# Where hidden tiles lie and in which order contraction tiles are taken, in a two-layer RetNet and GLA trunk

## The chip, the cores and the metric

The kernel runs on one core of one Trainium2 chip. The metric is the device time of an execution in microseconds, the median of several runs.

## The reference

A trunk of two layers on 512 tokens of width 1024, with 16 learned meta tokens ahead of them (528 columns). Each layer is a half-step SwiGLU FFN (hidden width 2816), a mixer, and another half-step FFN, each behind an RMSNorm; layer 0 mixes by retention (4 heads, keys of 256, values of 512), layer 1 by gated linear attention (GLA). Cut to what matters here:

```python
for i in range(2):
    h = h + 0.5 * swiglu(rmsnorm(h, norm_ffn1[i]), ffn1_w_in[i], ffn1_w_out[i])
    hn = rmsnorm(h, norm_mix[i])
    h = h + (retention(hn, ...) if i == 0 else gla(hn, ...))
    h = h + 0.5 * swiglu(rmsnorm(h, norm_ffn2[i]), ffn2_w_in[i], ffn2_w_out[i])

def swiglu(x, w_in, w_out):
    gate, up = split(x @ w_in, 2)
    return (silu(gate) * up) @ w_out

def retention(h, w_in, head_norm, w_out):       # per head, decayed and causal
    q, k, v, g = split(h @ w_in)
    q, k = rotary(q), rotary(k) / 16
    o = rmsnorm(((q @ k.T) * decay) @ v, head_norm)
    return (o * silu(g)) @ w_out
```

## The kernel before

Everything lies transposed: channels on the 128 partitions, the 528 tokens in the free dimension, in two halves of 264. A "row tile" is 128 channels.

Every product is made in float32r from split operands. `mm3` (L472) issues three matmuls for one contraction tile: the weight's high part with the moving operand's high and low part (L473, L474), then the weight's low part with the high part again (L475). A matmul has a 128x128 weight and 264 moving columns (256 in the last FFN). Weights come from HBM, and ACT and DVE split each into high and low part some tiles ahead (L167, L168).

Most projections are made as "units": two row tiles of the output and two token halves by a Strassen-like scheme of seven products instead of eight. `unit_steps` (L667) issues them in the order of `Weights.UNIT` (L75), each over the contraction tiles that `ks` names, in the order given. The moving operand of a product is either a quarter of the input itself (n11, n21, n22) or a precomputed sum of quarters (t1, t2, n3, t4):

```python
    UNIT = ("a11", "s1", "s2", "a12", "s3", "s4", "a22")
    WITH = {"a11": ("n11", "X"), "s1": ("t1", "Z"), "s2": ("t2", "X"), "a12": ("n21", "Q"), "s3": ("n3", "X"),
            "s4": ("n22", "Z"), "a22": ("t4", "X")}
```

X is a PSUM bank that several products of a unit use one after another, with an ACT copy of it in between; Q and Z are the two banks of one accumulator.

An input projection contracts over 4 pairs of row tiles, so a product has 4 x 3 = 12 matmuls and a unit 84. Its inputs are u (`Split`, L401; quarters at a pitch `HP_` of 288 floats, k after k) and the sums in `th`, `tl` (L768 to L770 in an FFN, L1209 to L1211 in the retention; `[P, 4, 4, 288]`, the slot ahead of the contraction tile). `FLIP` (32 floats) lies between high and low parts. `rows4` (L709) gives the contraction tiles as 0, 1, 2, 3.

An FFN makes hidden row tiles in pairs (f, f+1), in three groups (`GROUPS`, L30): f = 0 to 6, 8 to 12, 14 to 20, so 4, 3 and 4 hidden tiles; the last FFN has four groups. A hidden tile holds seven quarters high and seven low. `h_tile` (L778) places it in one of four buffers H0 to H3, by a count of the tiles made so far. `hidden` (L823) fills it from the gated rows; for f = 0 and 2 it is put off (`todo`, L1041 to L1049), so that in the FFNs with three groups the tiles of the first group are made in the order f = 0, 4, 2, 6. H0 to H3 also hold, at the start of an FFN, temporary sums (H0, H1) and the normalized and gated rows of f = 0 and 2 (H2, H3; `place`, L783). `unit_o` (L981) is a unit of a group's out product; it sorts the group's tiles by f, and contracts over them as 0, 1, 2, 3, or, where the group has four tiles and the product's slot is odd, as `ODD` = 1, 0, 3, 2 (L59, L987). The out product of a group runs after the first gate unit of the next.

The retention (L1200) runs head by head: q and k (`rope`, units but in head 0), the out product of the head before, the values (`rv`, units but in head 0), scores and transposes, gates (`rg`, two units in every head), and the product with the values (`pv`). The out product, `out_steps` (L1062), makes 8 row tiles, each in two token halves over 4 contraction tiles (the four value tiles of the head), plain, without sums: 8 x 2 x 4 x 3 = 192 matmuls. Its input `og` has a pitch of 288 floats between halves and 608 between contraction tiles (L1476). The last head's is made with `part=2`: the first two row tiles take their first two contraction tiles before all else.

The framework's scheduler fixes the order of instructions on each engine when the kernel is built, from program order and priorities (`urgent`, L450); on the chip each engine runs its own list in order.

Of the kernel before, what the change touches and what calls it, by code (L numbers as in the profile page):

```python
# [11 lines left out]
F32R = mybir.dt.float32r  # L12
# [4 lines left out]
P = 128  # L17
# [16 lines left out]
HALVES = ((0, 264), (264, 528))  # L34
# [24 lines left out]
ODD, BACK = (1, 0, 3, 2), 48  # L59
# [180 lines left out]
def trunk(ctx, tc, a):  # L240
# [8 lines left out]
    W = Weights(tc, ctx)  # L249
# [200 lines left out]
    def urgent():  # L450

        return tc.high_priority(offset=HEAD_START)
# [183 lines left out]
    def width(halves):  # L636
        return halves[0][1] - halves[0][0]
# [71 lines left out]
    def rows4(what):  # L709
        return range(4)  # L710

    def unit(key, name, order, halves, ks, rhs, place, row1, c22, c21, behind=None):
        wd = width(halves)

        def places():
            X = bank(f"X{name}")[:, :wd]
            QZ = acc_tile(f"QZ{name}")[:, :, :wd]
            su = place()
            return X, QZ, su[:, :2], su[:, 2:]

        for st in unit_steps(key, name, order, halves, ks, rhs, places, row1, c22, c21, behind):
            st()
# [30 lines left out]
    def ffn(which, layer, halves, gcol, u, feed, late=False):  # L753


        me = f"{which}{layer}"
# [4 lines left out]
        with tc.tile_pool(name=f"h_{me}", bufs=1) as hp, tc.tile_pool(name=f"t_{me}", bufs=1) as tp, \  # L761
# [3 lines left out]
            HW = 14 * pitch + flip  # L765
# [5 lines left out]
            places = [lambda i=i: tp.tile([P, 4, HT], F32, tag=f"t{i}", name=f"sz{me}") for i in "hl"]  # L771
            th, tl = [[t[:, :, k, :wd] for k in range(4)] for t in (th, tl)]
            rhs_in = quarters(halves, u, th, tl)
            H, normed, made = {}, {}, [0]
            place_of = [spare() if feed else in_turn([lambda: tp.tile([P, 4, wd], F32, tag="su", name=f"su{me}", bufs=3)])]
            groups = GROUPS if feed else LAST_GROUPS

            def h_tile(name):  # L778

                made[0] += 1  # L780
                return hp.tile([P, HW], F32R, tag=f"H{(made[0] - 1) % 4}", name=name)

            def place(j):  # L783

# [38 lines left out]
            def hidden(f, y, part=None):  # L823

                gi = [g[0] <= f < g[1] for g in groups].index(True)
                if feed is None and gi == len(groups) - 1:
                    h = h_tile(f"h{me}{f}")[:, BACK:]
                    h = [[h[:, q * 2 * wd:q * 2 * wd + T] for q in (i, i + 2)] for i in (0, 1)]
                    h = [list(t) for t in zip(*h)]
                    for i in range(2):  # L830
                        split(pair(h[0][i], halves), pair(h[1][i], halves), y[:, 2 - 2 * i:4 - 2 * i])
                elif part == 1:
                    (hi, lo), t = h, _ = halfway.pop()
                    with urgent():
                        split(hi[:, :2], lo[:, :2], y[:, :2])
                    V.tensor_sub(t[0][:, 0], y[:, 1], y[:, 3])
                    split(hi[:, 3], lo[:, 3], t[0][:, 0])
                    V.scalar_tensor_tensor(t[1][:, 1], y[:, 0], -1.0, t[1][:, 0], ALU.mult, ALU.subtract)
                    split(hi[:, 6], lo[:, 6], t[1][:, 1])
                else:  # L840
                    h = h_tile(f"h{me}{f}")
                    hi, lo = h = [h[:, o:o + 7 * pitch].rearrange("p (q t) -> p q t", q=7)[:, :, :wd]
                                  for o in (0, 7 * pitch)]
                    t = t_pair(tmp, ("hf", "hf"), f"{me}h{f}", wd)
                    if part is None:
                        t_sums(t, y[:, 1:3], y[:, 3], y[:, 0])
                        split(hi[:, :3], lo[:, :3], y[:, :3])
                        for i in range(2):
                            split(hi[:, 3 + 2 * i:5 + 2 * i], lo[:, 3 + 2 * i:5 + 2 * i], t[i])
                    else:  # L850
                        with urgent():

                            split(hi[:, 2], lo[:, 2], y[:, 2])
                            V.tensor_sub(t[0][:, 1], y[:, 2], y[:, 3])
                            split(hi[:, 4], lo[:, 4], t[0][:, 1])
                            V.scalar_tensor_tensor(t[1][:, 0], y[:, 1], -1.0, t[0][:, 1], ALU.mult, ALU.subtract)
                            split(hi[:, 5], lo[:, 5], t[1][:, 0])
                        halfway.append((h, t))
                H.setdefault(gi, {})[f] = h
# [29 lines left out]
            turn = [0]  # L889
# [125 lines left out]
            for n, (kind, a_, b_) in enumerate(steps):  # L1015
                if kind == "p":
                    s, f = a_, b_
# [44 lines left out]
    def out_steps(name, key, hh, hl, halves, scale, feed, per=1, part=None):  # L1062


        nk, wd = len(hh), width(halves)
        ws, ps = {}, {}

        def products(d, k0, k1):
            if d // per not in ws:
                ws[d // per] = W.get(key(d // per))  # L1070
            if k0 == 0:
                ps[d] = acc_tile(f"po_{name}{d}")
            for hf, (r0, r1) in enumerate(halves):
                for k in range(k0, k1):
                    mm3(ps[d][:, hf, :wd], *W.at(ws[d // per], ((d % per) * nk + k) * P),
                        hh[k][:, r0:r1], hl[k][:, r0:r1], k == 0, k == nk - 1)
                if k1 == nk:
                    if hf == len(halves) - 1 and d % per == per - 1:
                        W.free(ws[d // per])
                    hook()  # L1080

        def step(d):
            if part and d == 0:
                for i in range(2):
                    products(i, 0, part)
            products(d, part if part and d < 2 else 0, nk)
            xv = x[d][:, halves[0][0]:halves[-1][1]].rearrange("p (b t) -> p b t", t=wd)
            with urgent():
                ins = V.scalar_tensor_tensor(xv, ps[d][:, :len(halves), :wd], scale, xv, ALU.mult, ALU.add)
            if feed:  # L1090
                feed(d, ins)

        return [lambda d=d: step(d) for d in range(KD)]
# [106 lines left out]
    def retention(u, feed):  # L1200
        with tc.tile_pool(name="retp", bufs=1) as rp, tc.tile_pool(name="wmore", bufs=2) as wp, psum_pool(4) as pp:
# [11 lines left out]
            rhs_u = quarters(HALVES, u, th, tl)  # L1213
            place = spare()
            causal = rp.tile([P, P], F32, tag="causal", name="causal")
            nc.sync.dma_start(causal, a["tri"][1])
            og, normed, tabs = {}, {}, {}
# [32 lines left out]
            def head(h):  # L1250
                qk = {}

                def rope_pair(s):


                    t = [(rp if s == "k" else tmp).tile([P, T], F32, tag=f"gs{m}" if s == "k" else "sg",
                                                        name=f"rt{s}{h}{m}") for m in range(2)]

                    def row1(ab, qz):
                        V.tensor_add(pair(t[0], HALVES), ab, qz)  # L1260

                    def c22(c, s_):
                        V.tensor_add(t[1][:, b0:b1], c, s_)

                    def c21(c):
                        S.copy(t[1][:, a0:a1], c)

                    j = (0 if s == "q" else 8) + 2 * h
                    unit(("rqk", j), f"rqk{s}{h}", W.UNIT, HALVES, rows4, rhs_u, place, row1, c22, c21)
                    cos, sin = [tabs[s][:, c, :] for c in range(2)]  # L1270
                    pa, pb = [tmp.tile([P, T], F32, tag="hf", name=f"r{i}{s}{h}") for i in "ab"]
                    V.tensor_mul(pa, t[0], cos)
                    V.tensor_mul(t[0], t[0], sin)
                    V.tensor_mul(pb, t[1], sin)
                    V.tensor_add(pa, pa, pb)
                    qk[s, 0], qk[s, 1] = [[rp.tile([P, T], F32R, tag=f"{s}{i}{m}", name=f"{s}{i}{m}_{h}")
                                           for i in range(2)] for m in range(2)]
                    S.copy(qk[s, 0][0], pa)
                    V.tensor_mul(t[1], t[1], cos)
                    V.tensor_sub(t[0], t[0], t[1])  # L1280
                    V.tensor_sub(qk[s, 0][1], pa, qk[s, 0][0].bitcast(F32))
                    split(qk[s, 1][0], qk[s, 1][1], t[0])
# [35 lines left out]
                def values():  # L1318
# [18 lines left out]
                    for m0 in (0, 2):  # L1337
                        vt.extend(rp.tile([P, T], F32, tag=f"gs{m0 + i}", name=f"vt{h}{m0 + i}") for i in range(2))

                        def row1(ab, qz, m0=m0):  # L1340
                            V.scalar_tensor_tensor(pair(vt[m0], HALVES), ab, -1.0, qz, ALU.mult, ALU.subtract)

                        def c22(c, s, m0=m0):
                            V.tensor_add(vt[m0 + 1][:, b0:b1], c, s)

                        def c21(c, m0=m0):
                            S.copy(vt[m0 + 1][:, a0:a1], c)

                        unit(("rv", h, m0), f"rv{h}{m0}", W.UNIT, HALVES, rows4, rhs_u, place, row1, c22, c21)

                def turn(j):
                    if not v:
# [61 lines left out]
                def gates(m0, use):  # L1414
# [16 lines left out]
                        S.activation(o, c, AF.Silu)  # L1431
                        use(m0 + 1, a0, a1, o)

                    unit(("rg", h, m0), f"rg{h}{m0}", W.UNIT, HALVES, rows4, rhs_u, place, row1, c22, c21)
                    sgs.extend(mine)

                def pv(into):
# [782 lines left out]
```

## Time and profile before

| | |
|---|---|
| median of 3 runs | 2061.5 us (2060.38 to 2062.69) |
| profiled execution | 2058.71 us |
| its span, first to last instruction | 2056.9 us |
| granted TensorE clock, mean | 0.997 |
| PE busy | 2030.9 us, 99% |
| DVE busy | 1795.5 us, 87% |
| ACT busy | 1199.0 us, 58% |

The page lists busy time by engine over one profiled execution. PE is the matmuls, PEld the weight loads that overlap them. Successive matmuls overlap too, each showing about 0.28 us from its start to its modelled end while they start some 0.12 us apart: "busy" says that PE has work, not that it works at its best. A timeline row has the start in us from the span's start, the duration, engine, source line, operation, and written and read tiles. A row of the table of windows has the stretch, its length, then each engine's busy time and number of instructions in it, the granted clock, and the share and rate of DMA.

### The profile page before, as it was taken

The numbers are of one execution on the slowest core, as the hardware profiler recorded it, in microseconds if no ns is written. First come the engines' busy times: TensorE is split into PE (matmuls) and PEld (weight loads), VectorE is DVE, ScalarE is ACT, GpSimd is POOL, SyncE is SP. The second block draws the span as 40 slices with busy tenths as digits, with TensorE's granted clock in tenths as the row PEclk, the third lists the DMA queues.
The fourth block names the chain that finished last, engine by engine and source line by source line (L and its number), as shares of the span: only waits on it lengthen the run. The fifth ranks groups of instructions, "written<-read, shape, count | busy, mean of one in ns | idle before, by whom it ended". The sixth has DMA issues, their size and how long they took to land. (4 is left out here: it accounts for less than half of the span.)

```text
span 2056.9 us, 43086 instructions
## 1 busy us (share of the span) xinstructions
PE 2030.9 (99%) x16335; PEld 1973.7 (96%) x16335; DVE 1795.5 (87%) x3299; ACT 1199.0 (58%) x2435; POOL 210.4 (10%) x181
## 2 busy tenths in 40 slices
PE   8999999999999999999999999999999999999998
PEld 8999999999999999999999999999999988999998
DVE  8988999978787889988889998999997968999996
ACT  5656666554545465656666665666745445666664
POOL 1011110010101000111111011111001000111110
PEclk9999999999999999999999999999999999999999
DMA  6576776455555532776776377677614351686872
GB/s 203 155 188 169 188 186 169 139 134 144 140 140 136 142 107 68 187 190 153 196 204 170 95 198 182 153 204 180 199 53 123 89 165 58 161 214 171 194 180 73
DMA packets 176112, 318.85 MB, mean 155 GB/s; under 512 B 17568, under 2 KB 40736, under 8 KB 175904
## 3 DMA queue, kind: packets, MB, share of 16 engines
q1 hardware_dynamic: 133856, 237.04, 35.3%
q0 software_dynamic: 40896, 75.51, 23.4%
q10 hardware_dynamic: 1152, 3.55, 0.5%
q8 instruction: 128, 2.10, 0.4%
q14 instruction: 80, 0.66, 0.1%
HBM read 311.76 MB, written 4.26 MB: 154 GB/s over the span
## 5 line engine op out<-in xcount | busy, mean ns | idle before, releaser
L167 ACT CAST whi<-raw 128x512 fp32r<-128x512 f32 (+1 forms) x893 | 525.3, 606 | 458.6 <-DVE raw L173 107.0
L168 DVE TENSOR_TENSOR wlo<-raw,whi 128x512 fp32r<-128x512 f32 (+1 forms) x893 | 586.2, 670 | 136.0 <-ACT whi L167 120.0
L167 ACT CAST whi<-pair 128x512 fp32r<-128x512 f32 (+1 forms) x304 | 183.9, 605 | 95.4 <-ACT su L695 12.7
L168 DVE TENSOR_TENSOR wlo<-pair,whi 128x512 fp32r<-128x512 f32 (+1 forms) x304 | 202.1, 665 | 5.8 <-ACT whi L167 5.0
L136 POOL DMA_DIRECT2D pair<-in_f_in x73 | 89.0, 1220 | 729.6 <-DVE wlo L168 333.4
L173 DVE TENSOR_TENSOR raw<-pair,raw 128x512 f32<-128x512 f32 (+1 forms) x146 | 97.4, 667 | 2.6
L175 DVE TENSOR_TENSOR raw<-raw,raw 128x512 f32<-128x512 f32 (+1 forms) x146 | 97.3, 667 | 2.5
L136 POOL DMA_DIRECT2D pair<-in_f_out x44 | 53.5, 1216 | 367.6 <-DVE wlo L168 120.5
L474 PE MATMUL po_r<-ogl,whi 128*128 128x264 f32 x256 | 72.1, 281 | 0.0
L473 PE MATMUL po_r<-ogh,whi 128*128 128x264 f32 x256 | 72.0, 281 | 0.0
L475 PE MATMUL po_r<-ogh,wlo 128*128 128x264 f32 x256 | 71.7, 280 | 0.0
L136 POOL DMA_DIRECT2D pair<-in_ret_in x20 | 24.4, 1222 | 297.6 <-DVE wlo L168 102.6
L473 PE MATMUL Xf10o<-hf,whi 128*128 128x264 f32 x176 | 50.7, 288 | 0.9 <-DVE x L1003 0.3
L473 PE MATMUL Xf20o<-hf,whi 128*128 128x264 f32 x176 | 50.6, 287 | 0.7 <-DVE x L1003 0.3
L473 PE MATMUL Xf11o<-hf,whi 128*128 128x264 f32 x176 | 50.4, 286 | 0.7 <-ACT hf L506 0.3
L474 PE MATMUL Xf10o<-hf,whi 128*128 128x264 f32 x176 | 49.5, 281 | 0.0
L474 PE MATMUL Xf20o<-hf,whi 128*128 128x264 f32 x176 | 49.5, 281 | 0.0
L474 PE MATMUL Xf11o<-hf,whi 128*128 128x264 f32 x176 | 49.5, 281 | 0.0
L475 PE MATMUL Xf10o<-hf,wlo 128*128 128x264 f32 x176 | 49.2, 281 | 0.0
L475 PE MATMUL Xf20o<-hf,wlo 128*128 128x264 f32 x176 | 49.2, 280 | 0.0
L475 PE MATMUL Xf11o<-hf,wlo 128*128 128x264 f32 x176 | 49.1, 280 | 0.0
L473 PEld LDWEIGHTS po_r<-ogh,whi 128*128 128x128 f32 x256 | 48.1, 188 | 0.0
(1172 smaller groups left out, 8515.6 us busy)
## 6 DMA issues: line engine op xcount, KB each, us to landing
raw<-in_f_in SPq DMA_DIRECT2D x277, 256.0 KB, 4.0
pair<-in_f_in SPq DMA_DIRECT2D x150, 256.0 KB, 4.3
pair<-in_f_in POOLq DMA_DIRECT2D x73, 512.0 KB, 6.8
raw<-in_f_out SPq DMA_DIRECT2D x80, 256.0 KB, 3.6
raw<-in_ret_in SPq DMA_DIRECT2D x76, 256.0 KB, 3.5
raw<-in_f_out SPq DMA_DIRECT2D x72, 192.0 KB, 3.2
pair<-in_f_out SPq DMA_DIRECT2D x48, 256.0 KB, 3.8
pair<-in_f_out POOLq DMA_DIRECT2D x24, 512.0 KB, 6.0
```

The costliest lines, as they stand in the source:

```text
L136: nc.gpsimd.dma_start(t, aps[2].unsqueeze(1).broadcast_to([P, 2, n]), accum_op=ALU.add)
L167: self.nc.scalar.copy(hi[:, :n], raw)
L168: V.tensor_sub(lo[:, :n], raw, hi[:, :n].bitcast(F32))
L173: V.tensor_add(s2, self.tiles[c][:, 1], self.tiles[c, "a11"])
L175: V.tensor_add(raw, raw, s2)
L473: nc.tensor.matmul(ps, lhsT=lh, rhs=rh, start=start, stop=False, **kw)
L474: nc.tensor.matmul(ps, lhsT=lh, rhs=rl, start=False, stop=False, **kw)
L475: return nc.tensor.matmul(ps, lhsT=ll, rhs=rh, start=False, stop=stop, **kw)
```

## The change

Three things. A hidden tile's buffer follows its row tile, `f // 2 % 4`, instead of a count of tiles made. Units of the retention take the contraction tiles in the order 1, 0, 3, 2 in the four products whose moving operand is a sum (t1, t2, n3, t4). And an out product with four contraction tiles takes them as 1, 0, 3, 2 in its second token half. Only the retention's has both; GLA's has one half.

```diff
     def rows4(what):
         return range(4)
 
+    def rows4_odd(what):
+        return range(4) if what[0] == "n" and what != "n3" else ODD
+
...
-            H, normed, made = {}, {}, [0]
+            H, normed = {}, {}
...
-            def h_tile(name):
+            def h_tile(f):
 
-                made[0] += 1
-                return hp.tile([P, HW], F32R, tag=f"H{(made[0] - 1) % 4}", name=name)
+                return hp.tile([P, HW], F32R, tag=f"H{f // 2 % 4}", name=f"h{me}{f}")
...
-                    h = h_tile(f"h{me}{f}")
+                    h = h_tile(f)
...
             for hf, (r0, r1) in enumerate(halves):
-                for k in range(k0, k1):
+                turn = ODD if hf and nk == len(ODD) else range(nk)
+                for k in turn[k0:k1]:
                     mm3(ps[d][:, hf, :wd], *W.at(ws[d // per], ((d % per) * nk + k) * P),
-                        hh[k][:, r0:r1], hl[k][:, r0:r1], k == 0, k == nk - 1)
+                        hh[k][:, r0:r1], hl[k][:, r0:r1], k == turn[0], k == turn[-1])
...
-                    unit(("rqk", j), f"rqk{s}{h}", W.UNIT, HALVES, rows4, rhs_u, place, row1, c22, c21)
+                    unit(("rqk", j), f"rqk{s}{h}", W.UNIT, HALVES, rows4_odd, rhs_u, place, row1, c22, c21)
```

The units `rv` (L1349) and `rg` (L1434) change in the same way as `rqk` (L1269).

More of the change, by code (lines that the diff above doesn't have):

```diff
@@ L826, in hidden @@
                 if feed is None and gi == len(groups) - 1:
-                    h = h_tile(f"h{me}{f}")[:, BACK:]
+                    h = h_tile(f)[:, BACK:]
                     h = [[h[:, q * 2 * wd:q * 2 * wd + T] for q in (i, i + 2)] for i in (0, 1)]
@@ L1347, in c21 @@
                             S.copy(vt[m0 + 1][:, a0:a1], c)
-                        unit(("rv", h, m0), f"rv{h}{m0}", W.UNIT, HALVES, rows4, rhs_u, place, row1, c22, c21)
+                        unit(("rv", h, m0), f"rv{h}{m0}", W.UNIT, HALVES, rows4_odd, rhs_u, place, row1, c22, c21)
                 def turn(j):
@@ L1432, in c21 @@
                         use(m0 + 1, a0, a1, o)
-                    unit(("rg", h, m0), f"rg{h}{m0}", W.UNIT, HALVES, rows4, rhs_u, place, row1, c22, c21)
+                    unit(("rg", h, m0), f"rg{h}{m0}", W.UNIT, HALVES, rows4_odd, rhs_u, place, row1, c22, c21)
                     sgs.extend(mine)
```

## The prediction

> **What bounds the kernel now.** The page first: one line for the span and one for each engine's share of it.
>
> ```profile
> span 2056.9 us, 43086 instructions
> PE 2030.9 (99%) x16335; PEld 1973.7 (96%) x16335; DVE 1795.5 (87%) x3299; ACT 1199.0 (58%) x2435; POOL 210.4 (10%) x181
> ```
>
> PE is busy 99% of the span, so time comes off the end only where the matmuls themselves get closer together or a stop of PE goes. The profiled execution took 2058.7 us, 1.8 more than its span and 2.8 (0.14%) less than the median of the three runs, 2061.5. I make the sum as a difference against the profiled execution and carry it over to the median.
>
> A busy PE is not a PE at its best. The matmuls of a stage overlap, so what counts is the distance between starts, and the table of windows gives it: a window's length over the matmuls in it (the count in brackets has two or three more, which only reach into the window; I use the program's own count). I asked for the first head's value projection, the first out product of the retention, three value stages made of products of sums, the first-group out products of two FFNs, and a second-group one.
>
> ```profile
> core 0: us, PE busy (x) PEld busy (x) DVE busy (x) ACT busy (x) POOL busy (x), PEclk, DMA share, GB/s
> 385.35:407.75 22.40, 22.40 (x194) 22.40 (x193) 22.38 (x42) 11.88 (x25) 0.00 (x0) 1.00 0.20 63
> 468.34:491.22 22.88, 22.88 (x194) 22.88 (x193) 22.32 (x37) 7.82 (x15) 0.00 (x0) 1.00 0.27 87
> 491.22:511.19 19.97, 19.97 (x171) 19.97 (x169) 15.00 (x23) 11.05 (x23) 2.44 (x2) 1.00 0.72 189
> 592.44:612.40 19.96, 19.96 (x170) 19.96 (x169) 14.99 (x23) 11.05 (x23) 2.44 (x2) 1.00 0.73 188
> 694.01:713.98 19.97, 19.97 (x171) 19.97 (x170) 14.55 (x23) 11.19 (x23) 2.44 (x2) 1.00 0.72 178
> 874.41:914.97 40.56, 40.56 (x339) 40.56 (x338) 34.48 (x58) 21.97 (x43) 4.87 (x4) 1.00 0.77 192
> 975.23:1006.23 31.00, 31.00 (x254) 30.50 (x253) 27.67 (x55) 19.03 (x42) 3.66 (x3) 1.00 0.77 199
> 1218.31:1258.87 40.56, 40.56 (x339) 40.56 (x338) 34.48 (x58) 21.97 (x43) 4.87 (x4) 1.00 0.75 191
> ```
>
> All of these are 128x264 matmuls at a granted clock of 1.00. The first row is the yardstick: 192 matmuls (4 tiles, 2 halves, 8 contraction tiles, 3 each) in 22.40 us, 116.7 ns each, with DVE busy for 22.38 of it. The out product below has the same 192 matmuls of the same form, PE is busy all through, and it takes 22.88: 0.48 us more without a stop. A value stage, two units of 7 x 4 x 3 = 84 matmuls, should take 168 x 0.1167 = 19.60 and takes 19.97: 0.37 more. An out product of a first group, four units, should take 336 x 0.1167 = 39.20 and takes 40.56: 1.36 more.
>
> The timeline shows where such time lies. First a change of product in an FFN unit, then the start of the fourth row of the out product (24 matmuls a row from 468.34), then, in the second head's k unit, the product with u that follows one with the sums.
>
> ```profile
> 302.61 0.28 PE L474 MATMUL QZf10g<-ulf,whi 128*128 128x264 f32 x1
> 302.72 0.28 PE L475 MATMUL QZf10g<-uhf,wlo 128*128 128x264 f32 x1
> 302.84 0.28 PE L473 MATMUL Xf10g<-thf,whi 128*128 128x264 f32 x1
> 302.96 0.28 PE L474 MATMUL Xf10g<-tlf,whi 128*128 128x264 f32 x1
> ```
>
> ```profile
> 476.57 0.28 PE L473 MATMUL po_r<-ogh,whi 128*128 128x264 f32 x1
> 476.69 0.28 PE L474 MATMUL po_r<-ogl,whi 128*128 128x264 f32 x1
> 476.81 0.28 PE L475 MATMUL po_r<-ogh,wlo 128*128 128x264 f32 x1
> 476.92 0.28 PE L473 MATMUL po_r<-ogh,whi 128*128 128x264 f32 x1
> ...
> 478.02 0.28 PE L473 MATMUL po_r<-ogh,whi 128*128 128x264 f32 x1
> ```
>
> ```profile
> 563.60 0.28 PE L473 MATMUL QZrqkk<-uhret,whi 128*128 128x264 f32 x1
> ...
> 564.93 0.28 PE L475 MATMUL QZrqkk<-uhret,wlo 128*128 128x264 f32 x1
> 565.15 0.39 PE L473 MATMUL Xrqkk<-rth,whi 128*128 128x264 f32 x1
> 565.38 0.29 PE L474 MATMUL Xrqkk<-rtl,whi 128*128 128x264 f32 x1
> ```
>
> The FFN unit goes from u to t without a break. In the out product the starts are 0.117 apart up to 476.92, and the next nine distances take 1.10 instead of 1.05 us. The eleven distances of the k unit's product take 1.33 instead of 1.28. Nothing waits there; the matmuls are only further apart for a while.
>
> **What sets it.** The code's constants offer a reason. A quarter's pitch is 288 floats, 1152 bytes, or four and a half times 256; hi and lo parts lie a further 128 bytes askew; an H tile is 14 x 288 + 32 floats, again an odd number of 128 bytes. So every step from hi to lo, from one contraction tile to the next, and from one H tile to the next moves the start of PE's moving operand into the other 128-byte half of a 256-byte stretch. Call the halves A and B. I write down the halves in program order and count the places where one matmul starts in the half of the one before ("repeats").
>
> In the value projection of the first head and in FFN units (sums and u begin in the same half) there is none, and their rows are clean. In the out product, half 0 of a row runs A B A B over its four contraction tiles (within a tile A B A), half 1 lies one pitch on and runs B A B A: a repeat between the halves and one between rows, 2 x 8 = 16 a head, and 0.48 / 16 = 30 ns each. In a retention unit the sums must begin in the half in which u ends: then u to t1, t2 to u, u to n3, n3 to u, u to t4 and t4 to the next u repeat, 6 a unit, and 0.37 / 12 = 30 ns each. The same price out of two different stages is what makes me believe the counting. The third place is a first group. Its H tiles are made in the order f = 0, 4, 2, 6 and lie in H0 to H3 in that order, so sorted by f their halves are A A B B: two repeats in each product, 14 a unit, and with the odd slots' order 1, 0, 3, 2 four more between products, 18 a unit, 72 an FFN, and 1.36 / 72 = 19 ns each where they crowd.
>
> **The change, part by part.** It adds and removes no instruction; the same matmuls read other places or come in another order.
>
> *H tiles by row tile.* f = 0, 2, 4, 6 now lie in H0, H1, H2, H3: A B A B, and the odd slots, by 1, 0, 3, 2, as well. No repeat is left in 72. Group 1 has H0 to H2 and group 2 H3, H0, H1, H2 both before and after, and the last FFN makes its tiles in the order of f anyway, so there nothing moves. FFNs with this first group: three (layer 0's two, layer 1's first). Two rows show 1.36 each; the third has the same 336 matmuls and I give it the same: 3 x 1.36 = 4.08 us.
>
> *Products of sums in the retention.* t1, t2, t4 and n3 by 1, 0, 3, 2: where the sums begin in B, their products now start in A and end in B as those of u do. Heads 1 to 3 have six units each, head 0 two: 20 units x 6 x 30 ns = 3.65 us (20 x 0.37 / 2 is 3.7). All four sums are ready before the first unit, so the order opens no wait.
>
> *Second half of the retention's out product.* 1, 0, 3, 2 gives A B A B in both halves: 4 x 0.48 = 1.92 us. In the last head the first two rows take two contraction tiles ahead of the rest; the slice 1, 0 is the same pair, and the last tile to be ready (m = 3, first token half) is asked for in half 0 first, before and after. GLA's last out product also has four contraction tiles but a single half, and is not touched.
>
> Sum: 4.08 + 3.65 + 1.92 = 9.65 us.
>
> *What waits take back.* Heads 1 to 3 have stops in the q and k units, as at 564.93 above, where PE stands for its X bank until ACT has copied it. If such a stop goes back to work that DVE and ACT began at the end of the product before, PE only arrives earlier and stands longer, and repeats removed ahead of it are lost: up to the q unit's 6 and the k unit's 4, 0.3 us a head, 0.9 in all; if it moves along with PE, nothing. I take the 0.9, since these stages follow the busiest of DVE. The out product itself is safe: DVE's 22.32 us fit into the 22.40 that remain, and the first row above shows PE at full pace beside 22.38. In the first groups DVE goes from 34.48 / 40.56, 85%, to 34.48 / 39.20, 88%.
>
> Sum with that: 9.65 - 0.9 = 8.75 us. Profiled execution 2058.7 to 2049.95, median 2061.5 to 2052.75; I say 2052.7.
>
> The Trainium skill speaks against the whole of this: "SBUF — State Buffer", section "Who interferes with whom", gives PE two independent read ports, one for the moving operand and one for weight loads, and calls the port pair shared by VectorE and GpSimd the only place of contention; the order of contraction tiles would then be worth 0. This trace parts from it in the second row against the first.
>
> **The rivals.**
>
> *Stops come in place of the repeats* (chance 0.13). The second-group row is the model: 252 matmuls should take 29.40 us, 12 repeats add 0.36, and it takes 31.00, so 1.24 is stops, at DVE 27.67 / 31.00 = 89%. The first groups come to 88%. If they stopped as often, 1.24 x 336 / 252 = 1.65 each, 5.0 in all would go: 8.75 - 5.0 = 3.75, so 2057.7; in between where fewer come. Against it: the second group's hidden tiles are made right ahead of it with a narrower margin, and at 85% the first groups of two FFNs have no stop at all.
>
> *No effect* (0.05). The lost time would belong to something that stays, such as the change of the PSUM bank or weight tile at the start of a product: 2061.5. Every slow place above does lie behind such a change. Against it: the FFN unit at 302.84 and the value projection change both without a break. This is also where that section on SBUF would have it end.
>
> *Slower* (0.04). Gated tile f = 4 now goes to H2, where the normalized rows and the gated rows of f = 0 lie; its writing has to wait until the first hidden tile has been made from them, and ACT's weight casts, on which PE lives, are queued behind. It decides if that wait exceeds 8.75 / 3 = 2.9 us an FFN. At half a unit, 4.9 us, it gives 3 x 4.9 - 8.75 = +6, so 2067.5.
>
> ```profile
> 827.71 0.70 DVE L507 TENSOR_TENSOR hf<-t1f20h,hf 128x528 fp32r<-128x528 f32 x1
> 844.95 0.86 ACT L506 CAST hf<-su 128x792 fp32r<-128x792 f32 x1 [0.69 <-DVE su L970]
> ```
>
> The first row ends the tile of f = 0, the second begins that of f = 4, 16.5 us later. With such room I give it little; most of the 0.04 is an order of instructions that comes out otherwise.
>
> **How the numbers follow.** 0.78 for the sum, 0.13, 0.05 and 0.04 for the rivals. The forecast is the likeliest case. Its own lower end: nothing taken back, 2051.85, less the 1.1 us by which the fastest run lies under the median, 2050.7; I say 2050.5. The upper end goes into the first rival, to 2057.3, nearly its 2057.7. Outside lie 0.05 + 0.04, half of the first rival and a little of the first case, together under 0.2. A change under 0.2%, 4.1 us, can't be told from none here: the bound lies at 2057.4. Faster 0.78 and most of the first rival, 0.87; same 0.05 and the rest of it, 0.09; slower 0.04.
>
> **What would show it.** Right: the out products of the retention at 22.4 us each, first groups at 39.2, value stages at 19.6, the boundaries in the timeline as even as that at 302.84, and each later stage starting earlier by what has been saved so far. The first rival: those distances even, but new gaps of 0.2 us or more at X banks in the first groups. Wrong: 22.88 and 40.56 as before (then the halves are not the cause), or value stages above 19.97 (then the sums begin in the same half as u, and the new order makes the repeats that it should remove).

## The result, and the profile after

The changed kernel takes 2054.7 us in the median of five runs (2050.3 to 2055.6), the kernel before 2061.5, so 6.8 us less in the medians. The ratio, which is not that of the medians, is 0.9963 with a 95% interval of 0.9949 to 0.9978, 7.6 us. Two further sets of runs gave 0.9959 (0.9947 to 0.9972) each, 7.9 and 8.2 us in the medians. Its profiled execution has a span of only 3.1 us less than that of before, 2053.8 against 2056.9, although the matmuls' distances have gained three times as much. Both have to be explained. The page's first lines have the same instructions and the same work for DVE, and 4.8 us less of busy PE:

```profile
span 2053.8 us, 43086 instructions
PE 2026.1 (99%) x16335; PEld 1968.4 (96%) x16335; DVE 1794.8 (87%) x3299; ACT 1198.9 (58%) x2435; POOL 210.3 (10%) x181
```

First the distances. These are the windows of the changed kernel for the same eight stages, in the same order, as those quoted of the kernel before:

```profile
382.59:404.99 22.40, 22.40 (x194) 22.40 (x193) 22.38 (x42) 11.89 (x25) 0.00 (x0) 1.00 0.19 60
468.21:490.61 22.40, 22.40 (x194) 22.40 (x193) 22.26 (x37) 7.82 (x15) 0.00 (x0) 1.00 0.25 83
490.61:510.21 19.60, 19.60 (x170) 19.60 (x169) 15.06 (x24) 11.05 (x23) 2.44 (x2) 1.00 0.75 190
590.25:609.85 19.60, 19.60 (x171) 19.60 (x169) 15.11 (x24) 11.05 (x23) 2.44 (x2) 1.00 0.72 186
690.53:710.13 19.60, 19.60 (x170) 19.60 (x169) 14.45 (x23) 11.19 (x23) 2.44 (x2) 1.00 0.72 183
869.88:909.15 39.27, 39.27 (x338) 39.27 (x337) 34.05 (x58) 21.91 (x43) 4.87 (x4) 1.00 0.77 195
969.41:1000.41 31.00, 31.00 (x255) 30.54 (x254) 27.70 (x55) 19.07 (x42) 3.66 (x3) 1.00 0.77 201
1213.86:1253.12 39.26, 39.26 (x338) 39.26 (x337) 34.05 (x58) 21.89 (x43) 4.87 (x4) 1.00 0.79 202
```

The yardstick and the second group stay (22.40, 31.00); the retention's out product has gone from 22.88 to 22.40, each value stage from 19.97 to 19.60, the first groups from 40.56 to 39.27. That is 116.7 ns a matmul everywhere, to within 0.1 us. The timeline at the start of the fourth row of the out product, where nine distances had taken 1.10 us, now has nine in 1.05:

```profile
476.50 0.28 PE L475 MATMUL po_r<-ogh,wlo 128*128 128x264 f32 x1
476.61 0.28 PE L473 MATMUL po_r<-ogh,whi 128*128 128x264 f32 x1
...
477.66 0.28 PE L473 MATMUL po_r<-ogh,whi 128*128 128x264 f32 x1
```

Then what was taken back. The granted clock is 0.995 in this profile, 0.997 in that of before. The windows table finds it: PE ran at half clock for 6.8 us between the first head's scores and gates, and for 3.4 us at two later places at the start of a stage. The first row is the window ahead of the half-clock stretch; the last column but two is the granted clock.

```profile
404.99:412.20 7.21, 5.59 (x44) 5.20 (x43) 7.18 (x17) 6.37 (x16) 1.23 (x1) 1.00 0.67 150
412.20:419.00 6.80, 6.71 (x34) 6.54 (x33) 4.76 (x13) 2.90 (x11) 0.00 (x0) 0.50 0.09 16
1118.80:1122.20 3.40, 3.40 (x17) 3.40 (x17) 1.93 (x6) 0.62 (x1) 1.92 (x2) 0.50 0.85 220
1463.50:1466.90 3.40, 3.40 (x13) 2.92 (x12) 2.44 (x6) 1.77 (x3) 1.73 (x2) 0.51 1.08 245
```

In the kernel before, the scores and gates of the first head ran at full clock all through:

```profile
407.75:416.94 9.19, 7.15 (x58) 6.61 (x57) 8.90 (x21) 7.52 (x20) 1.23 (x1) 1.00 0.58 123
416.94:436.96 20.02, 20.02 (x172) 20.02 (x169) 14.98 (x28) 12.22 (x26) 1.23 (x1) 1.00 0.49 134
```

There the two stages take 29.21 us; in the changed kernel they take from 404.99 to 436.64, 31.65, so 2.4 us are lost although the gates lost their repeats. Setting the start of each stage in one trace against the other gives the account of the two profiled executions: first groups 2.57 + 1.29 + 1.30 = 5.2 us won, out products 1.8, value stages 1.1, q and k units 0.4, gates of heads 1 to 3 0.8, in all 9.3; head 0's scores and gates lose 2.4, the starts of two later stages 1.4 and 2.5, in all 6.3. The other stages differ both ways and about cancel (the most, 1.6 us, is won in the first FFN's plain up products, where the kernel before ran at half clock at 21 us); what is left, 3.0, is the difference of the spans, 3.1, to within 0.1.

### The profile page after: what moved, and what is told of

Its sections match the earlier page's. It is cut to its first block, busy times and chain, and to the rows that moved or that the text cites. A ratio compares the mean times of both kernels' runs of the same rounds, so it can differ in the third digit from the quotient of the medians.

```text
span 2053.8 us, 43086 instructions
## 1 busy us (share of the span) xinstructions
PE 2026.1 (99%) x16335; PEld 1968.4 (96%) x16335; DVE 1794.8 (87%) x3299; ACT 1198.9 (58%) x2435; POOL 210.3 (10%) x181
## 4 chain that ended last, share of the span: by engine, by line
PE 75%; DVE 16%; ACT 3%; issue 3%; DMA 2%; POOL 0%; SPq 0%; POOLq 0%; DVEq 0%; ACTq 0%
DVE wlo L168 5%; PE po_r L474 1%; PE po_r L475 1%; PE po_r L473 1%; ACT whi L167 1%; DVE hf L507 1%; PE Xf21o L473 1%; PE lv L1753 1%; PE Xf20o L473 1%; PE Xf20o L474 1%; PE Xf20o L475 1%; DVE unf L799 1%; PE Xf21o L475 1%; PE Xf21o L474 1%; PE Xf11u L473 1%
## 5 line engine op out<-in xcount | busy, mean ns | idle before, releaser
L474 PEld LDWEIGHTS po_r<-ogl,whi 128*128 128x128 f32 x256 | 48.0, 188 | 0.0
```

Of the source, the lines that this page charges most:

```text
L474: nc.tensor.matmul(ps, lhsT=lh, rhs=rl, start=False, stop=False, **kw)
```

## The experiments

The theory: a repeat of the 128-byte half costs 19 to 30 ns and the change removes some 400 of them (3 x 72 in the first groups, 20 x 6 in the units, 4 x 16 in the out products, by the prediction's count). The rivals: the loss belongs to the change of product, bank or weight (the prediction's "no effect"); the order of the weights, not the operand's place, makes the difference; or stops and half clock set the time. Every kernel is timed against the kernel before, with the ratio's 95% interval. Unless it says otherwise, nothing of the computation is left out.

**One part at a time, on the kernel before.** First the tiles: `h_tile(f)` with `tag=f"H{f // 2 % 4}"`, and nothing else of the diff.

> The kernel before with one part of the change: hidden tiles placed by their row tile. Theory (a repeat of the 128-byte half costs 19 to 30 ns): the out products of the three first groups go from 40.56 us to 39.2 where they had no stop, everything else keeps its distances (value stages 19.97, retention out products 22.88); 4.1 us under the kernel before at the same clock, and 5.2 if the 1.1 us of stops in the first FFN's first group go as well, as they did in the changed kernel. Rival (the stops and the new buffers, not the halves): only the first FFN's group gets shorter, by 1.1, and the other two stay at 40.56.

Ratio 0.9982 (0.9973 to 0.9991), 3.5 us less in the medians. The first groups of the first and the second FFN in this kernel:

```profile
113.51:152.71 39.20, 39.20 (x339) 39.20 (x337) 34.27 (x58) 21.73 (x43) 4.87 (x4) 1.00 0.73 193
872.13:911.39 39.26, 39.26 (x338) 39.26 (x337) 34.04 (x58) 21.89 (x43) 4.87 (x4) 1.00 0.73 189
```

All of 40.56 to 39.2 comes from this part alone, and the first FFN's group, 41.77 before, loses its stops too: 5.2 us by distances. Value stages (19.97) and out products (22.88) stay. The profile has 3.4 us of half clock at 413 us, which made the first head's scores and gates 30.8 us for 29.2. So 5.2 - 1.6 = 3.6, and 3.5 were measured. The rival of stops alone falls: two groups without any stop got shorter.

The second part alone: `rows4_odd` in `rqk`, `rv` and `rg`.

> The kernel before with one part of the change: products of sums in the retention by 1, 0, 3, 2. Theory (repeats): each value stage goes from 19.97 to 19.60 us, the units of q, k and gates lose 0.18 each where no stop takes it back; 2.5 to 3.6 us under the kernel before. Rival (stops that are set by DVE and ACT take most of what is won outside the value stages): 1.1 us from the value stages and little more, 1.1 to 1.5 in all.

0.9989 (0.9980 to 0.9998), 1.9 us. The first of its value stages:

```profile
490.38:510.02 19.64, 19.64 (x170) 19.64 (x169) 14.93 (x23) 11.05 (x23) 2.44 (x2) 1.00 0.70 183
```

19.64 and not 19.60, because the out product ahead of it still ends in the half in which the units begin. Gates win their share (19.65 to 19.38 us in heads 1 and 2), the q units 0.3 us of the 0.5 expected, and the k units 0.4 to 0.8, depending on which profile of the kernel before they are set against. The size lies between theory and rival, and its interval, 0.4 to 4.1 us, holds both. Half clock at 1465 us in its profile may be one reason; that is not shown for the median.

The third part alone: the second half's `turn` in `out_steps`.

> The kernel before with one part of the change: the second token half of the retention's out product by 1, 0, 3, 2. Theory (repeats): the four out products go from 22.88 to 22.40 us, 1.9 us under the kernel before, which five rounds can just tell. Rival (DVE is full in this stage, 22.3 of 22.9 us): 22.88 stays, or gaps come in it, 0 to 0.5 us.

0.9991 (0.9982 to 0.9999), 1.9 us, as the theory said. Its first out product:

```profile
467.87:490.32 22.45, 22.45 (x194) 22.45 (x193) 22.28 (x37) 7.82 (x15) 0.00 (x0) 1.00 0.28 95
```

DVE's 22.28 us fit into 22.45 and make no gap. The three parts sum to 7.4 us in the medians, the change gave 7.6 to 8.4 by its ratios.

**The two kernels again.** Unchanged copies, for further profiles.

> The kernel before, unchanged, to see what two sets of runs of one kernel differ by and whether stretches of half clock come at other places in another profile. If those stretches fall by chance of an execution, this profile has a different set of them from the first profile of the same kernel (there: two, both in the first 55 us) and its span moves by up to 3 us with them; if they belong to a place of the program, it has the same two. Ratio to the kernel before: 1.000 within 0.0015.

1.0000 (0.9992 to 1.0009). This profile has one stretch of 3.4 us at 50.6 us and none in the middle.

> The changed kernel again, to have a second profile and five more pairs. Theory (9.3 us come from the matmuls' distances, and the first profile of the changed kernel lost about 6 of them to stretches of half clock in the middle): distances as in the first profile (22.40, 19.60, 39.2), stretches of half clock at other places, 6 to 9 us under the kernel before. Rival (the stretches in the middle come from the change): the same three stretches again, near 410, 1118 and 1463 us.

0.9959 (0.9947 to 0.9972). Half clock for 6.8 us at 411 us again, but none at 1118 and 1463. The first head's scores and gates:

```profile
404.02:414.15 10.13, 8.44 (x58) 7.92 (x57) 9.56 (x22) 7.51 (x20) 1.23 (x1) 0.85 0.50 116
414.15:435.61 21.46, 21.46 (x170) 21.46 (x169) 14.35 (x27) 11.99 (x26) 1.23 (x1) 0.91 0.44 126
```

31.59 us, the same loss. So the two later stretches come and go, and the one behind the scores does not, in this kernel.

**Order or place?** The changed kernel with the order turned in all products of the retention's units:

```diff
     def rows4_odd(what):
-        return range(4) if what[0] == "n" and what != "n3" else ODD
+        return ODD
```

> The changed kernel with 1, 0, 3, 2 in all seven products of the retention's units, those with u too. Theory (repeats): the sums run A to B and u now B to A, so all 116 repeats of these units are back and the value stages take 19.97 us as before the change; 2.5 to 3.6 us over the changed kernel. Rival (the order 1, 0, 3, 2 is cheaper in itself, by the weights' places or the PSUM bank): 19.60 stays, no loss.

0.9977 (0.9967 to 0.9987), 2.9 us over the changed kernel's run in the same set, and the first value stage is back:

```profile
490.72:510.68 19.96, 19.96 (x171) 19.96 (x169) 15.06 (x24) 11.09 (x23) 2.44 (x2) 1.00 0.73 193
```

And the opposite: plain order for the weights, the sums laid out the other way.

```diff
-        return range(4) if what[0] == "n" and what != "n3" else ODD
+        return range(4)
...
-            th, tl = [[t[:, :, k, :HT] for k in range(4)] for t in (th, tl)]
+            th, tl = [[t[:, :, ODD[k], :HT] for k in range(4)] for t in (th, tl)]
```

> The changed kernel with the plain order 0, 1, 2, 3 in all products of the retention's units, but with the sums of contraction tile k lying at place 1, 0, 3, 2 in their tile. The moving operands start in the same halves one after the other as in the changed kernel, while weights are taken as before the change. Theory (repeats): value stages 19.60, the same time as the changed kernel. Rival (the order of the weights): 19.97 in each value stage, 2.5 to 3.6 us over the changed kernel.

0.9953 (0.9940 to 0.9965), no slower than the changed kernel, and:

```profile
489.00:508.60 19.60, 19.60 (x170) 19.60 (x169) 15.04 (x24) 11.05 (x23) 2.44 (x2) 1.00 0.73 192
```

One kernel has the new order and the old time, the other the old order and the new time. Only the places at which successive moving operands begin go with the time; order as such, weights and banks do not. The tiles-only kernel says the same of the first groups, for it moves buffers and leaves every order within a product as it was. For the out product no such pair was made.

**A dose the other way.** `rows4_odd` in the FFNs' input units too, where it makes repeats.

> The changed kernel with the order 1, 0, 3, 2 for sums in the input units of the FFNs as well, where sums and u begin in the same half: it makes the repeats there that it takes away in the retention. Theory (repeats): 6 in each of the 56 units of the three FFNs with 264 columns, some 330 by 30 ns, 10 us over the changed kernel; the last FFN, whose 256 columns end where they begin and which repeats everywhere already, stays as it is. Rival (order alone, or a switch of product): no loss, or the same loss a unit in the last FFN too.

0.9967 (0.9956 to 0.9978), 2.2 us over the changed kernel in the same set, not 10. The second FFN's gate and up units for f = 10, in the changed kernel and then in this one:

```profile
918.47:928.51 10.04, 10.04 (x87) 9.91 (x86) 9.95 (x18) 6.52 (x13) 1.20 (x1) 1.00 0.69 169
928.51:938.71 10.20, 10.12 (x87) 9.91 (x86) 8.08 (x15) 6.35 (x13) 1.23 (x1) 1.00 0.80 202
```

```profile
918.35:928.33 9.98, 9.98 (x87) 9.98 (x85) 9.90 (x18) 6.51 (x13) 1.20 (x1) 1.00 0.67 168
928.33:938.64 10.31, 10.30 (x86) 10.10 (x85) 8.13 (x15) 6.42 (x13) 1.23 (x1) 1.00 0.77 201
```

The repeats are there: the gate unit has gone from 9.80 us of matmuls and a stop of 0.24 to 9.80 + 6 x 0.03 = 9.98 and no stop. DVE is busy 9.95 of 10.04 us in it, so the gate unit is probably set by DVE, and what PE loses comes out of its stop. DVE's share alone doesn't tell, for the retention's out product is nearly as full of DVE (22.32 of 22.88 us before the change), has no stop, and paid for every repeat. In the up unit, DVE at 8.1 us, 0.11 of the 0.18 shows. Over the whole profile the 27 gate units take 271.9 us, as in the changed kernel (271.9 to 272.2 in three profiles), and the up units of the three FFNs 2.0 us more than there (297.8 against 295.6 to 296.0): that is the loss of 2.2. The theory's count held and its price did not: in the gate units, which had a stop to give up, a repeat cost nothing. In the last FFN, where the rival wanted the same loss, the input units take 188.5 us against 187.6 to 188.1 in the changed kernel and 187.9 to 188.9 in two profiles of the kernel before, and no 0.18 each shows.

I first took it otherwise: 21 of 27 gate units had a stop at their last product (the expectation below says 22), and 18 of these were gone, so perhaps that stop was missed by a few ns and cost a refill of PE. That can be tested with two repeats around n22, the product during which the bank has to be read; the function below takes the place of `rows4` in the gate units of the three FFNs:

```diff
+    def rows4_gate(what):
+        return ODD if what == "n22" else range(4)
```

> The changed kernel with 1, 0, 3, 2 in one product, that of n22, of the gate units of the three FFNs with 264 columns. It makes two repeats a unit on purpose (into n22 and out of it), 54 in all. In the kernel where the FFN units were given six repeats each, 22 of 27 gate units had lost the stop of some 0.22 us at their last product, whose bank VectorE must have read while n22 runs. Theory (that stop is missed by less than the two repeats make n22 longer, and costs a refill of PE however short the wait): the stops of gate units go, 22 x 0.22 = 4.8 us, for 54 x 30 ns = 1.6: 2 to 3.2 us under the changed kernel. Rival (repeats only add, the stops went there because all six slowed the unit, so that VectorE and ScalarE caught up): stops stay, 1 to 1.6 us over the changed kernel.

0.9957 (0.9944 to 0.9971), against 0.9959 of the changed kernel in the same set; by the medians it is 1.1 us over it (2051.6 against 2050.5), which intervals this wide can't tell from nothing. The stops stay, and so does the unit:

```profile
917.67:927.72 10.05, 10.05 (x87) 9.94 (x86) 9.96 (x18) 6.52 (x13) 1.20 (x1) 1.00 0.72 185
```

My theory of a stop missed by little falls. The rival said 1 to 1.6 us over the changed kernel, as the medians have it, but the gate units don't show it: the 27 take 272.2 us, within the 271.9 to 272.2 of the changed kernel. Two repeats vanish in a unit whose stop can take them up. In two gate units that had no stop (9.80 us) they show with their full price, 9.86.

**The half clock.** Six matmuls of ones in head 0's scores, ahead of those of the last block, in a bank that these overwrite; the results stay what they were.

```diff
-                        sc = bank(f"sc{h}{j}")[:n, :MR]
+                        sc = bank(f"sc{h}{j}")
+                        for _ in range(6 if h == 0 else 0):
+                            nc.tensor.matmul(sc.rearrange("p (n c) -> p n c", c=P), lhsT=ones_r,
+                                             rhs=ones_r.unsqueeze(1).broadcast_to([P, 4, P]), start=True, stop=True)
+                        sc = sc[:n, :MR]
```

> The changed kernel with six matmuls of ones added in head 0's score stage, into a bank that is overwritten after, to keep PE busy where it waits 1.7 us and where profiles of the changed kernel show PE's clock at half speed for 3.4 to 6.8 us just after. Theory (the half-clock stretch is set off by PE's idle time there and takes back 1.6 to 2.8 us of what the change won): no such stretch near 411 us in the profile, 1 to 2.5 us under the changed kernel. Rival (the stretch has another cause, or the added matmuls cost what they save): stretch stays, 0 to 1 us over the changed kernel.

0.9945 (0.9933 to 0.9958), 2047.5 us, 3.0 under the changed kernel's median in the same set. There is no half clock in the middle of the profile:

```profile
406.27:416.08 9.81, 8.37 (x65) 7.48 (x63) 9.54 (x22) 7.54 (x20) 1.23 (x1) 1.00 0.54 122
416.08:435.81 19.73, 19.73 (x170) 19.73 (x170) 14.39 (x27) 12.10 (x26) 1.36 (x2) 1.00 0.48 136
```

29.54 us for the two stages instead of 31.6, although the first is 0.6 longer than the 9.19 of the kernel before. The added matmuls don't fill the longest wait. It is 1.4 us by the trace, where the expectation has 1.7, and it is still there: they need the same bank and start behind it, two at 412.17 and four at 413.64. What is gone are the stops of 0.2 and 0.4 us that followed, and PE is busy for 8.37 of 9.81 us in the stage instead of 7.15 of 9.19.

> The changed kernel, unchanged, beside the other kernels of this call: what they are measured against, and a third set of pairs with the kernel before. 7 to 9.5 us under it; distances as before, a stretch of half clock in the score stage of head 0, as in both its profiles so far.

0.9959 (0.9947 to 0.9972), 8.2 us less in the medians, and half clock for 6.8 us at 411 us once more.

> The changed kernel with both additions, the n22 product of the gate units by 1, 0, 3, 2 and the matmuls of ones in head 0's score stage. If both theories hold, 3 to 5.5 us under the changed kernel and 11 to 14 under the kernel before; if only that of the stops holds, 2 to 3; if neither, 1 to 2.5 over the changed kernel.

0.9953 (0.9940 to 0.9966), 2049.1 us, no half clock in the middle. The n22 part brings the filled kernel nothing; it is 1.6 us over it in the medians. The best version is the filled one: its interval still overlaps that of the changed kernel, but the windows show where 2.1 us of it come from.

## Why the prediction was right, and where it was off

*The repeats.* Right, in place and price. Out products fell by 0.48 in heads 0 to 2, value stages by 0.37, first groups by 1.3, and in the units the two kernels that part order from place leave no other cause among those named. That the total came out so near is in part luck: the end of the first FFN's stops gave 1.2 us more than the sum had, half clock took 1.6 to 2.8 us that it did not have, and neither was foreseen.

*First groups, 4.08 us.* 5.2 in fact. The step said that the first FFN's group would win the same 1.36 as the others; it won 2.57, since its stops went too. The first and longest of three stops is at the third product, which must wait until X has been copied (L695) and starts 0.47 us after the matmul before it instead of 0.12. This is ACT in the kernel before, then the start of that product:

```profile
114.61 0.37 ACT L946 ACTIVATE gf<-Xf10g 128x264 f32<-128x264 f32 x1
116.20 0.63 ACT L167 CAST whi<-raw 128x512 fp32r<-128x512 f32 x1 [1.22 <-DVE raw L175]
116.73 0.37 ACT L695 COPY su<-Xf10o 128x264 f32<-128x264 f32 x1
117.15 0.39 PE L473 MATMUL Xf10o<-hf,whi 128*128 128x264 f32 x1 [0.19 <-ACT su L695]
```

The copy stands behind a weight cast that waits 1.22 us for DVE. With the new places, the copy no longer stands behind a cast that waits (in the tiles-only kernel it starts at 115.68, in a program that is 0.4 us ahead). The tile of f = 2 then goes to a buffer that is free earlier, so its casts can come sooner in ACT's list. The order of instructions differs by much else between the two, so that the stops go with the tiles is shown, and this path only likely.

*Units, 3.65 less 0.9.* 1.1 + 0.4 + 0.8 measured for heads 1 to 3, 2.3, and head 0's gates, 0.3 in the units-only kernel (20.02 to 19.73), are covered by half clock: near the 2.75. The q and k units won 0.4 of their 1.1, so 0.65 was lost where 0.9 was forecast. But the q units kept 0.3 of their 0.5, and the k units of the changed kernel take from 10.08 to 10.99 us in three profiles: that waits take back what repeats give is shown for some k units and not as a rule.

*Out products, 1.92.* 0.48 three times and 0.39 in the last head, 1.8: right.

*The rival of stops.* Not in the first groups, where it was placed. But the mechanism is real in the FFNs' input units, as the dose shows; had the change been made there, the sum would have been wrong by a factor of four to five (10 us against 2.2).

*What no step had.* The prediction took the clock as given; the row of the span and the windows at 1.00 had raised no doubt. Half clock behind head 0's scores takes 1.6 to 2.8 us: 9.6 us by distances, with head 0's gates, come out as 7.6 to 8.4. All eight profiles of kernels with the new tile places and without the added matmuls have such a stretch at 410 to 415 us, one of four with the old places has. The score stage itself is the same in both up to where the clock falls. All stretches of one profile begin a multiple of 3.41 us apart. With the new places the program ahead of the stage is some 2.6 us shorter, so it can fall otherwise on such a raster. No kernel shifted it alone, but the profiles can be sorted by it. The other stretches of a profile give the marks of its raster, and one of them falls between 1 and 4.4 us after the first score matmul:

| mark, after the first score matmul | profiles | half clock |
|---|---|---|
| 1.5 to 2.0 us | five: four with the new tile places, one with the old | 3.4 us |
| 2.3 to 2.7 us | three, all with the old | none |
| 3.3 to 3.8 us | four, all with the new | 6.8 us |
| 1.6 and 1.8 us, with the added matmuls | two, with the new | none |

So the stretch goes with where the stage falls on the raster, and not with the tile places as such. And the added matmuls did not just move the stage, for their two profiles lie where five others have the stretch. Two windows from mark to mark in the kernel with n22 turned, then in the filled one:

```profile
411.09:414.50 3.41, 2.06 (x16) 1.81 (x16) 3.15 (x8) 3.14 (x10) 0.00 (x0) 1.00 0.69 118
414.50:417.91 3.41, 3.41 (x18) 3.40 (x19) 3.07 (x9) 0.83 (x3) 0.00 (x0) 0.50 0.00 0
```

```profile
411.48:414.90 3.42, 2.73 (x16) 2.20 (x17) 3.42 (x8) 2.10 (x5) 0.00 (x0) 1.00 0.73 129
414.90:418.31 3.41, 3.41 (x32) 3.34 (x31) 2.98 (x10) 2.62 (x10) 0.00 (x0) 1.00 0.00 0
```

That PE's idleness sets the stretch off is borne out by these. How much idleness it takes is open: a window with PE busy for 2.13 us was not followed by half clock in the kernel before (410.09 us), and one with 2.30 was in the out-product-only kernel (411.61 us).

The Trainium skill, "SBUF — State Buffer", section "Who interferes with whom", calls one port pair of other engines the only place of contention, so by it the change would have had no effect; the trace disagrees, with 22.88 against 22.40 us for the same matmuls, and in the units the kernels that part order from place settle it. The Trainium skill, "TensorE: Matmul & The Clock Gate", section "What's actually happening", has a free-running activity window of about 3.4 us after which an idle PE is clocked at half; the stretches of 3.4 and 6.8 us agree, and so do their starts, multiples of 3.41 us apart. The Trainium skill's rule of thumb in the same page's section "HAM oscillation — how this bites in real kernels", no idle gap over about 3.4 us, does not: the longest gap of PE in that stage is 1.4 us.

## What to carry to other kernels

Divide a window's length by its matmuls before believing a busy PE: 119.2 ns where 116.7 are possible is 2% that no list of waits shows. Then ask who sets the pace of that stage: the same 30 ns was worth its full price where PE had no stop, and nothing in units with a stop of 0.24 us that could take it up. And look at the granted clock by stage: a phase of scattered short stops can cost another microsecond or two after it.

## What the runs showed of the hardware

When a 264-column moving operand begins in the same 128-byte half of a 256-byte stretch as the one before, PE falls behind by 30 ns in all where such places are well apart (0.48 us / 16), by 18 to 19 where they crowd (1.29 to 1.36 / 72), spread over the next matmuls. Only starts that lie whole multiples of 128 bytes apart were tried. In the last FFN, whose operands have 256 columns, every operand begins in the same half by the code's constants. Yet its input units start their matmuls 114.8 to 115.6 ns apart in the mean without stops, and some 113.3 all through (9.52 us for 84); 116.7 x 256 / 264 = 113.2 would be no loss at all (an estimate). So the start alone doesn't make the loss; that it is the start against where the operand before ended would fit, and no run changed the width alone. In both profiles with six matmuls of ones that nobody reads, behind the longest wait of a stage, PE's clock stayed up, and that stage and the next took 2.1 us less (29.5 against 31.6).
